# Softmax sums divided in four pieces from a copy, query projection by alternating column halves, and column-half matmuls kept together in the planned order

## Chip, cores and metric

One NeuronCore of one Trainium2 chip runs the whole program; the other cores do nothing. The metric is the device time of one execution in microseconds (us), median over several executions; smaller is better. Nothing of the computation is done on the host.

## What is computed

One step of a two-layer hybrid backbone over 1280 tokens (256 prompt, 1024 sample tokens), model width 1024, all in float32. Each layer makes one input projection, feeds eight heads of latent attention and four heads of a bidirectional gated delta rule, and joins both in one output projection:

```python
mod = jnp.dot(jax.nn.silu(cond), w_ada) + b_ada               # shift, scale, gate
h = rmsnorm(x, norm_w) * (1.0 + scale) + shift
z = jnp.einsum('bsd,de->bse', h, w_in)
q = jnp.einsum('bsr,rf->bsf', rmsnorm(q_lat, q_a_norm), w_qb)  # 8 heads, 64 + 32 wide
kv = jnp.einsum('bsr,rf->bsf', ckv_all, w_kvb)                 # 256 cached + 1024 sample keys
s = (q_nope . k_nope + q_pe . k_pe) * scale
o_a = softmax(s, axis=-1) . v * silu(g_a)
o_b = rmsnorm(o_forward + flip(o_reverse)) * silu(g_b)         # two scans in chunks of 64
x = x + gate * einsum(concat(o_a, o_b), w_out)
```

A scan step computes `v_new = u - w S`, `o = q S + intra v_new`, `S = S*gl + k^T v_new` for each head and direction. A final RMSNorm closes the step; the compressed keys and the scan states are outputs as well.

## The kernel before

**Order.** The program is written as many Python generators ("threads"). `Sched.run` plays them against estimates of each operation's time and always takes the operation that could start first; threads have priorities. What it records is the fixed order of every engine's instructions, so a changed cost or rule moves instructions all over the program. A helper records all operations, so nearly all have line 312 (315 after the change); names tell them apart. Where the plan leaves TensorE idle, `keep_warm` (L178) puts in matmuls that compute nothing, named `spare`.

**Column halves.** A matmul with at most 64 output rows takes a half of TensorE's columns; `Op.half` holds its first output row, 0 or 64 (for the conditioning product `adap` one of four quarters, 0, 32, 64, 96), and is None for a whole one. Once `run` has taken an operation, it goes on with the same thread while the next one's `half` is true and nothing blocks it (L131). `emit` charges 8 ns for a half whose predecessor used another half of the same tile (L267 to L276).

**Stages.** Each layer runs an input projection (`zp`, weights split in high and low parts, three products), in which the delta rule's matrices are prepared, then attention with the scan beside it, then the output projection (`wop`). In one layer's attention stretch every head h has two threads:

- `prep(h)` (L1461) projects keys (`kp`) and queries (`qp`, in `qproj`, L1490: two column blocks j into output rows 0 to 63 and 64 to 127 of one bank, two products k added up for each), takes the scores' maxima (`pm` on TensorE, reductions on VectorE), transposes them (`mxt`), has ScalarE negate them, and sends them through DRAM (`mx_d`) into one row of the query tile. Scores (`sp`) of that head wait for this row.
- `main(h)` (L1555) makes, for each block of 128 keys, the scores (`sp`), their exponentials on ScalarE (`pe`), and the product with the values (`po`), and adds the exponentials up in `acc`. GpSimd does most of these adds and VectorE some, the last one among them. After 2 blocks (prompt) and 10 blocks (sample) it starts a `finish` thread.
- `finish` (L1615) sums `acc` over partitions on TensorE (`pd`), takes the reciprocal into the tile `ob`, multiplies by the gate on GpSimd and by `po` on VectorE, and sends the result away. There are two `ob` tiles. It has 2 × 8 × 2 = 32 calls; half have 512 columns, half 128.

Beside them stand the scan (`ks`, `up`, `su`, `po<-S,kc` on TensorE; `ru`, `S`, `oT` on VectorE and ScalarE), the squares of its output (`jk` on ScalarE), the values of the next pair of heads (`vp` to `vv`), and the splitting of the output weights in high (`woh`, ScalarE) and low (`wol`, GpSimd) parts. In the code below, V is VectorE, S ScalarE, G GpSimd, PE TensorE, SY SyncE.

Of the kernel before, what the change touches and what calls it, by code (L numbers as in the profile page):

```python
# [16 lines left out]
P = 128  # L17
# [14 lines left out]
BLK = ((0, 256), (256, 512), (768, 512))  # L32
# [24 lines left out]
class Sched:  # L57
# [47 lines left out]
    def run(self):  # L105
        while self.th:
# [19 lines left out]
            r, _, t = best  # L126
            if t.q:
                if isinstance(t.q[0], Op):
                    self.t = t.t = max(t.t, t.q[0].start())
                Sched.step(t)  # L130
                while t.q and isinstance(t.q[0], Op) and t.q[0].half and not t.q[0].blocker():  # L131
                    Sched.step(t)
                continue
            t.t, t.wait = r, None
# [87 lines left out]
class Op:  # L222
# [44 lines left out]
    def emit(self):  # L267
        s = self.start()
        if self.eng == "PE":
            n = self.outs[0][0]  # L270
            if (self.half is None) != (Sched.half is None):
                s = max(s, Sched.clk.get("PE", 0.0) + (92 if Sched.half is None else 200))
            if self.half is not None:
                if Sched.half not in (None, (n, self.half)) and Sched.half[0] == n:
                    self.ns = 8
            Sched.half = None if self.half is None else (n, self.half)  # L276
        e = s + self.ns
        if self.eng == "PE":
            Sched.keep_warm(s)
# [115 lines left out]
def body(tc, I, O):  # L395
# [11 lines left out]
    PE, V, S, G, SY = Eng(nc.tensor, "PE"), Eng(nc.vector, "V"), Eng(nc.scalar, "S"), Eng(nc.gpsimd, "G"), Eng(nc.sync, "D")  # L407
# [6 lines left out]
    def bank(name):  # L414
        yield "bank"
        Sched.banks.remove(min(Sched.banks))
        t = pp.pool.tile([P, 512], F32, tag="mm", name=name)
        Sched.span(t)
        return t
# [139 lines left out]
    def mixer(l, hhl):  # L559
# [901 lines left out]
        def prep(h):  # L1461
# [27 lines left out]

            def qproj(bl):  # L1490
                pt = yield from bank("qp")
                for j, b in enumerate(bl):
                    c0, n = BLK[b]
                    for k in range(2):
                        PE.matmul(pt[64 * j : 64 * j + 64, :n], hw[:, k, :], qn[:, k, c0 : c0 + n], start=(k == 0), stop=(k == 1))
                yield 0
                for j, b in enumerate(bl):
                    c0, n = BLK[b]
                    S.copy(at["qr"][0:64, c0 : c0 + n], pt[64 * j : 64 * j + 64, :n])
                free(pt)  # L1500
                for b in bl:
                    c0, n = BLK[b]
# [112 lines left out]
        def finish(h, po, acc, m, c0, n, ga):  # L1615
# [4 lines left out]
            pd = yield from bank("pd")  # L1620
# [1 line left out]
                PE.matmul(pd[64 * x : 64 * x + 64, :n], twos, acc[:, x, :n])  # L1622
            yield 0
            ob = at["ob"][i % 2]
            V.reciprocal(ob[:, :n], pd[:, :n])
            free(pd)
            yield 0
            G.tensor_tensor(ob[:, :n], ga, ob[:, :n], op=ALU.mult)
            yield 0
            V.tensor_tensor(ob[:, :n], po[:, :n], ob[:, :n], op=ALU.mult)  # L1630
# [279 lines left out]
```

## Time and profile before

| what | us |
|---|---|
| median of 3 executions | 2223.09 (2219.53, 2223.09, 2223.38) |
| the profiled execution | 2217.9, of which the span 2216.1 |
| TensorE (PE) busy | 2097.0, 95% of the span, mean granted clock 0.986 |
| VectorE (DVE) busy | 1442.9 |
| GpSimd (POOL) busy | 847.4 |
| ScalarE (ACT) busy | 771.0 |

The span is the time from the first to the last recorded instruction of the profiled execution; 1.8 us of its time lie around it. Busy times are unions of an engine's intervals. Matmul intervals overlap, since they are pipelined. TensorE's records come singly for float32r matmuls and in pairs for float32 ones (`kp`, `qp`, `po`, `pd`, `spare`). The bracket at a timeline row's end gives the engine's idle time before it and what ended it.

### The profile page before, as it was taken

How to read it: one execution, taken by the hardware profiler on the slowest of the kernel's cores; microseconds unless marked ns; L12 is line 12 of the kernel's file. 1: busy time of each engine (PE TensorE's matmuls, PEld its weight loads, DVE VectorE, ACT ScalarE, POOL GpSimd, SP SyncE). 2: the span in 40 equal slices, each digit the busy share in tenths (PEclk: the TensorE clock that was granted, in tenths of full speed). 3: DMA queues.
4: the chain of work that ended last, by engine and by line, in shares of the span. 5: the costliest groups of instructions: out<-in, count | busy, mean ns of one | idle time of the engine just before them, and what ended most of it. 6: DMA issues, size and time to landing. Idle time of an engine off the chain costs nothing. (4 is left out here: it accounts for less than half of the span.)

```text
span 2216.1 us, 35036 instructions
## 1 busy us (share of the span) xinstructions
PE 2097.0 (95%) x12154; PEld 1519.9 (69%) x12154; DVE 1442.9 (65%) x3085; ACT 771.0 (35%) x2120; POOL 847.4 (38%) x757
## 2 busy tenths in 40 slices
PE   8899999989989998999999999998998999899998
PEld 6676778778666654555777777887876665455576
DVE  4767476686585765564667783887749576665454
ACT  4244224242124344443222441433222434544311
POOL 2343222352415247445331442144341524735521
PEclk9999999989999999999999999999999999999999
DMA  7376776856764322101423654677875441310153
GB/s 276 118 240 196 250 223 194 237 168 209 221 168 150 101 83 71 34 18 50 148 101 95 196 163 151 191 219 216 255 248 158 116 136 53 100 33 19 41 161 110
DMA packets 388481, 327.88 MB, mean 148 GB/s; under 512 B 88736, under 2 KB 326784, under 8 KB 388048
## 3 DMA queue, kind: packets, MB, share of 16 engines
q1 hardware_dynamic: 388304, 325.63, 48.9%
q8 instruction: 97, 1.59, 0.3%
q14 instruction: 80, 0.66, 0.1%
HBM read 220.08 MB, written 105.46 MB: 147 GB/s over the span
## 5 line engine op out<-in xcount | busy, mean ns | idle before, releaser
L312 PE MATMUL zp<-hh,wh 128*128 128x512 f32 (+2 forms) x1128 | 421.5, 374 | 8.4 <-DVE ai L312 6.9
L312 PE MATMUL zp<-hh,wl 128*128 128x512 f32 (+2 forms) x1128 | 421.1, 373 | 4.1 <-POOL wl L312 3.8
L312 PE MATMUL zp<-hl,wh 128*128 128x512 f32 (+2 forms) x1128 | 420.6, 373 | 3.2 <-POOL hl L312 3.1
L312 POOL TENSOR_TENSOR wl<-wr,wh 128x512 fp32r<-128x512 f32 (+1 forms) x114 | 156.2, 1370 | 400.8 <-DVE wh L312 231.5
L312 ACT ACTIVATE pe<-sp 128x512 f32<-128x512 f32 (+1 forms) x352 | 201.6, 578 | 259.0 <-PE sp L312 243.5
L312 DVE TENSOR_REDUCE at<-pm 128x1 f32<-128x512 f32 (+1 forms) x336 | 212.3, 683 | 80.2 <-PE pm L312 79.3
L312 POOL TENSOR_TENSOR pe<-pe,pe 128x1024 f32<-128x1024 f32 x96 | 229.3, 2388 | 80.8 <-DVE pe L312 51.4
L312 PEld LDWEIGHTS zp<-hh,wh 128*128 128x128 f32 (+1 forms) x1128 | 214.1, 190 | 41.9 <-DVE ai L312 7.1
L312 PE MATMUL sp<-at 97*128 97x512 f32 (+1 forms) x704 | 239.9, 408 | 2.6 <-ACT pe L312 1.5
L312 PEld LDWEIGHTS zp<-hh,wl 128*128 128x128 f32 (+1 forms) x1128 | 214.0, 190 | 38.0 <-issue 5.6
L312 PEld LDWEIGHTS zp<-hl,wh 128*128 128x128 f32 (+1 forms) x1128 | 214.2, 190 | 36.3 <-POOL hl L312 4.5
L312 PE MATMUL po<-pe,vv 128*64 128x512 f32 (+1 forms) x768 | 187.1, 563 | 3.4 <-ACT pe L312 2.6
L312 PEld LDWEIGHTS sp<-at 97*128 97x128 f32 x704 | 123.3, 189 | 88.5 <-issue 56.1
L312 POOL TENSOR_SCALAR kpt<-ktok,kdb 128x128 f32<-128x128 f32 x160 | 130.0, 824 | 94.1 <-DMA ai_d<-kpt 84.4
L312 PE MATMUL pm<-at 96*128 96x512 f32 (+1 forms) x416 | 129.2, 385 | 7.9 <-ACT at L312 4.6
L312 PE MATMUL sp<-at,at 97*128 97x512 f32 (+1 forms) x352 | 136.5, 388 | 0.0
L312 DVE TENSOR_TENSOR pe<-pe,pe 128x256 f32<-128x256 f32 (+1 forms) x64 | 79.5, 1244 | 83.9 <-POOL pe L312 43.4
L312 PE MATMUL wop<-woh,ol 128*128 128x512 f32 x288 | 114.4, 397 | 2.2 <-POOL ol L312 2.2
L312 PE MATMUL wop<-woh,oh 128*128 128x512 f32 x288 | 114.5, 398 | 0.0
L312 PE MATMUL wop<-wol,oh 128*128 128x512 f32 x288 | 114.3, 397 | 0.0
L312 PEld LDWEIGHTS pm<-at 96*128 96x128 f32 x416 | 70.9, 191 | 61.5 <-ACT pe L312 21.4
L312 DVE TENSOR_TENSOR wtmp<-blk,W 104x31 f32<-104x31 f32 (+15 forms) x248 | 105.6, 426 | 4.6 <-POOL W L312 0.9
(267 smaller groups left out, 3860.7 us busy)
## 6 DMA issues: line engine op xcount, KB each, us to landing
wr<-in_w_main SPq DMA_DIRECT2D x116, 256.0 KB
ti<-ai_d SPq DMA_DIRECT2D x144, 192.0 KB
ai_d<-ai SPq DMA_DIRECT2D x80, 256.0 KB
kc<-kqv_d SPq DMA_DIRECT2D x160, 128.0 KB
wa<-in_w_ada SPq DMA_DIRECT2D x64, 256.0 KB
kqv_d<-yc SPq DMA_DIRECT2D x48, 256.5 KB
kq<-kqv_d SPq DMA_DIRECT2D x16, 641.0 KB
rb<-grow_d SPq DMA_DIRECT2D x80, 128.0 KB
```

What stands on the lines that cost most here:

```text
L312: op = Op(lambda: f(*a, **k), self.key, self.ns(name, a, k, aps), outs, [x for x in aps if x is not acc])
```

## The change

```diff
--- before.py
+++ after.py
@@ -128,7 +128,7 @@
                 if isinstance(t.q[0], Op):
                     self.t = t.t = max(t.t, t.q[0].start())
                 Sched.step(t)
-                while t.q and isinstance(t.q[0], Op) and t.q[0].half and not t.q[0].blocker():
+                while t.q and isinstance(t.q[0], Op) and t.q[0].half is not None and not t.q[0].blocker():
                     Sched.step(t)
                 continue
             t.t, t.wait = r, None
@@ -270,10 +270,13 @@
             n = self.outs[0][0]
             if (self.half is None) != (Sched.half is None):
                 s = max(s, Sched.clk.get("PE", 0.0) + (92 if Sched.half is None else 200))
-            if self.half is not None:
-                if Sched.half not in (None, (n, self.half)) and Sched.half[0] == n:
-                    self.ns = 8
-            Sched.half = None if self.half is None else (n, self.half)
+            if self.half is None:
+                Sched.half = None
+            elif Sched.half and Sched.half[0] == n and self.half not in Sched.half[1]:
+                self.ns = 8
+                Sched.half[1].add(self.half)
+            else:
+                Sched.half = (n, {self.half})
         e = s + self.ns
         if self.eng == "PE":
             Sched.keep_warm(s)
@@ -1489,9 +1492,9 @@
 
             def qproj(bl):
                 pt = yield from bank("qp")
-                for j, b in enumerate(bl):
-                    c0, n = BLK[b]
-                    for k in range(2):
+                for k in range(2):
+                    for j, b in enumerate(bl):
+                        c0, n = BLK[b]
                         PE.matmul(pt[64 * j : 64 * j + 64, :n], hw[:, k, :], qn[:, k, c0 : c0 + n], start=(k == 0), stop=(k == 1))
                 yield 0
                 for j, b in enumerate(bl):
@@ -1622,9 +1625,12 @@
                 PE.matmul(pd[64 * x : 64 * x + 64, :n], twos, acc[:, x, :n])
             yield 0
             ob = at["ob"][i % 2]
-            V.reciprocal(ob[:, :n], pd[:, :n])
+            S.copy(ob[:, :n], pd[:, :n])
             free(pd)
             yield 0
+            for x in range(0, n, P):
+                V.reciprocal(ob[:, x : x + P], ob[:, x : x + P])
+                yield 0
             G.tensor_tensor(ob[:, :n], ga, ob[:, :n], op=ALU.mult)
             yield 0
             V.tensor_tensor(ob[:, :n], po[:, :n], ob[:, :n], op=ALU.mult)
```

Four things change. `run` keeps an operation with half 0 with its predecessor too (0 counted as false before). `emit` charges 8 ns only for a half that the running set has not used yet. `qproj` has the product index outside the block index, so halves alternate 0, 64, 0, 64. `finish` copies the sums to SBUF on ScalarE, frees the bank, and takes the reciprocal there in place, in pieces of 128 columns, between which other threads may go.

Over the whole program TensorE's order gets 50 more `spare` instructions (231 for 181), VectorE's 80 reciprocals of these for 32, ScalarE's 32 copies more; GpSimd's and SyncE's counts stay. The order on every engine is another one. Three places follow.

**GpSimd, layer 0**, late in attention, where a head's adds end; the stretch begins with adds of `pe` into the sum. Before:

```order
L312 TENSOR_TENSOR pe_8841<-pe_8841,pe 128x1024
L312 TENSOR_TENSOR wol_9020<-wor,woh_9019 128x512
L312 TENSOR_TENSOR pe_8841<-pe_8841,pe 128x1024
L312 TENSOR_TENSOR wol_9020<-wor,woh_9019 128x512
L312 TENSOR_TENSOR wol_9035<-wor,woh_9034 128x512 x2
L312 TENSOR_TENSOR wol_9051<-wor,woh_9050 128x512 x2
L312 TENSOR_TENSOR ob_7082<-at_7080,ob_7082 128x512
```

After:

```order
L315 TENSOR_TENSOR pe_9180<-pe_9180,pe 128x1024
L315 TENSOR_TENSOR wol_9193<-wor,woh_9192 128x512
L315 TENSOR_TENSOR pe_9180<-pe_9180,pe 128x1024
L315 TENSOR_TENSOR wol_9224<-wor,woh_9223 128x512 x2
L315 TENSOR_TENSOR wol_9259<-wor,woh_9258 128x512 x2
L315 TENSOR_TENSOR wol_9307<-wor,woh_9306 128x512 x2
L315 TENSOR_TENSOR wol_9364<-wor,woh_9363 128x512 x2
L315 TENSOR_TENSOR ob_7094<-at_7092,ob_7094 128x512
```

Behind the last add stood five `wol` in a row; now there are eight. VectorE's order beside it (adds of `pe`, the next head's maxima `at_6488` from `pm`) was:

```order
L312 TENSOR_TENSOR pe_8841<-pe_8841,pe 128x1024
L312 TENSOR_REDUCE at_6488<-pm 128x1 x4
L312 TENSOR_REDUCE at_6488<-pm 128x2
L312 TENSOR_REDUCE at_6488<-at_6488 128x8
L312 TENSOR_TENSOR pe_8841<-pe_8841,pe 128x1024 x2
```

and now is:

```order
L315 TENSOR_REDUCE at_6488<-pm 128x1
L315 TENSOR_TENSOR pe_9180<-pe_9180,pe 128x1024
L315 TENSOR_REDUCE at_6488<-pm 128x1 x3
L315 TENSOR_REDUCE at_6488<-pm 128x2
L315 TENSOR_TENSOR pe_9180<-pe_9180,pe 128x1024
L315 TENSOR_REDUCE at_6488<-at_6488 128x8
```

The maxima of the next head were all reduced ahead of this head's last two adds; now four reductions stand between these adds and the one that ends the maxima stands behind both.

**TensorE, layer 0**, where one head's scores end and the next head's (`sp` of 256 columns) begin; `mxt` starts the way of the next head's row of maxima. Before:

```order
L312 MATMUL mxt<-ident,at_6488 10x128
L312 MATMUL sp<-at_6486 128x512
L312 MATMUL sp<-at_6486,at_6487 128x512
L312 MATMUL sp<-at_6486 128x512 x2
L312 MATMUL sp<-at_6486,at_6487 128x512
L312 MATMUL po<-pe,vv 64x512 x2
L312 MATMUL sp<-at_6486 128x512 x2
L312 MATMUL sp<-at_6486,at_6487 128x512
L312 MATMUL sp<-at_6486 128x512 x2
L312 MATMUL sp<-at_6486,at_6487 128x512
L312 MATMUL po<-pe,vv 64x512 x4
L433 MATMUL spare<-ident 128x128
L312 MATMUL pd<-pe_10143,twos 64x512 x2
L312 MATMUL sp<-at_7079 128x256 x2
```

After:

```order
L315 MATMUL sp<-at_6486 128x512 x2
L315 MATMUL sp<-at_6486,at_6487 128x512
L315 MATMUL mxt<-ident,at_6488 10x128
L315 MATMUL po<-pe,vv 64x512 x4
L315 MATMUL pd<-pe_10179,twos 64x512 x2
L436 MATMUL spare<-ident 128x128 x5
L315 MATMUL sp<-at_7091 128x256 x2
```

The transposition has moved behind all scores of the old head. Between it and the new head's scores stand `po`, `pd` and five `spare` in place of scores, products and one `spare`.

**ScalarE, layer 1**, the end of the scan, where `jk` squares its output and TensorE wants exponentials (`pe`) and keys (the casts from `kp`). Before:

```order
L312 COPY ru<-up 128x128 x2
L312 ACTIVATE pe<-sp 128x512
L312 ACTIVATE jk,o_19057<-oT 128x128 x9
L312 COPY vv<-vp 128x512
L312 ACTIVATE jk,o_19057<-oT 128x128
L312 COPY vv<-vp 128x512
L312 ACTIVATE pe<-sp 128x512
L312 COPY vv<-vp 128x512
L312 ACTIVATE pe<-sp 128x512
L312 CAST at_17391<-kp 64x384 x2
L312 ACTIVATE pe_19125<-sp 128x2x128
```

After:

```order
L315 COPY ru<-up 128x128 x2
L315 CAST at_17452<-kp 64x384 x2
L315 ACTIVATE jk,o_19171<-oT 128x128 x9
L315 COPY ob_17455<-pd 128x512
L315 ACTIVATE jk,o_19171<-oT 128x128
L315 CAST at_17452<-kp 64x384 x2
L315 ACTIVATE pe_19157<-sp 128x2x128
L315 ACTIVATE pe<-sp 128x2x128
```

And what TensorE has beside it after the change:

```order
L315 MATMUL po<-S_19100,kc 128x128
L315 MATMUL pd<-pe_18600,twos 64x512 x2
L315 MATMUL sp<-at_16839 128x256 x2
L315 MATMUL sp<-at_16839,at_16840 128x256
L315 MATMUL kp<-at_16838,at_16841 64x384 x2
L315 MATMUL sp<-at_16839 128x256 x2
L315 MATMUL sp<-at_16839,at_16840 128x256
L436 MATMUL spare<-ident 128x128 x10
L315 MATMUL po<-pe_19157,vv 64x128 x2
L315 MATMUL po<-pe,vv 64x128 x2
L436 MATMUL spare<-ident 128x128 x10
L315 MATMUL otp<-ident,oT 128x128 x2
```

Ten squares and the copy `ob<-pd` now stand ahead of the exponentials `pe_19157`, which TensorE wants for `po`. The values' copies (`vv`) that stood between the squares are gone from here; two pairs of key casts surround the squares.

## Rows read from the trace of the kernel before

**Rows 1.** Busy time by stretch (stretch, its us; per engine busy, count; PEclk; DMA).

```profile
95.00:620.00 525.00, 495.85 (x3326) 391.41 (x3326) 356.06 (x906) 165.29 (x573) 180.03 (x216) 0.98 0.71 213
620.00:1047.00 427.00, 408.08 (x2120) 245.02 (x2120) 264.19 (x460) 184.19 (x404) 193.78 (x119) 0.99 0.29 82
...
1172.00:1690.00 518.00, 490.77 (x2982) 405.92 (x2981) 373.70 (x944) 167.50 (x573) 188.79 (x224) 0.99 0.65 193
1690.00:2105.00 415.00, 399.06 (x2028) 236.93 (x2028) 257.82 (x439) 176.69 (x386) 190.85 (x117) 0.98 0.27 77
...
844.30:846.30 2.00, 1.98 (x5) 0.37 (x5) 0.30 (x1) 0.00 (x0) 0.00 (x0) 0.50 0.01 4
```

**Rows 2.** Timeline, PE, query projections (start, us; count; idle and releaser in brackets).

```profile
701.99 1.08 PE L312 MATMUL qp<-at,at 128*64 128x256 f32 x4
...
705.99 1.94 PE L312 MATMUL qp<-at,at 128*64 128x512 f32 x8
707.87 0.50 PE L312 MATMUL sp<-at 97*128 97x512 f32 x1
```

**Rows 3.** By line and shape: the reciprocals of DVE and one copy of ACT.

```profile
L312 DVE RECIPROCAL ob<-pd 128x512 f32<-128x512 f32 x16 | 53.7, 3358 | 21.8 <-PE pd L312 21.6
...
L312 DVE RECIPROCAL ob<-pd 128x128 f32<-128x128 f32 x16 | 15.2, 953 | 7.4 <-PE pd L312 7.3
...
L312 ACT COPY vv<-vp 128x512 f32<-128x512 f32 x24 | 13.9, 585 | 17.9 <-PE vp L312 17.9
```

**Rows 4.** Timeline, DVE then PE, layer 1, a division beside the scan.

```profile
1788.29 3.36 DVE L312 RECIPROCAL ob<-pd 128x512 f32<-128x512 f32 x1
1791.56 0.77 DVE L312 SCALAR_TENSOR_TENSOR ru<-ks,neg_eg,vtok 128x128 f32<-128x128 f32 x3
...
1789.06 2.17 PE L433 MATMUL spare<-ident 128*128 128x128 f32 x18
1791.87 1.00 PE L312 MATMUL up<-ru,ti 128*128 128x128 f32 x6 [0.64 <-DVE ru L312]
```

**Rows 5.** Timeline, DVE, POOL, PE: one undisturbed sum, two beside GpSimd.

```profile
1785.81 1.22 DVE L312 TENSOR_TENSOR pe<-pe,pe 128x1024 f32<-128x1024 f32 x1
...
827.97 1.89 DVE L312 TENSOR_REDUCE at<-pm 128x1 f32<-128x512 f32 x3 [1.76 <-PE pm L312]
...
836.90 4.96 POOL L312 TENSOR_TENSOR wol<-wor,woh 128x512 fp32r<-128x512 f32 x4
...
836.98 5.96 DVE L312 TENSOR_TENSOR pe<-pe,pe 128x1024 f32<-128x1024 f32 x1 [6.92 <-POOL pe L312]
...
844.32 1.98 PE L312 MATMUL pd<-pe,twos 128*64 128x512 f32 x4 [5.47 <-DVE pe L312]
...
866.49 3.50 POOL L312 TENSOR_TENSOR at<-at,at 96x512 fp32r<-96x512 f32 x2
...
866.55 2.29 DVE L312 TENSOR_TENSOR pe<-pe,pe 128x1024 f32<-128x1024 f32 x1 [6.29 <-POOL pe L312]
```

**Rows 6.** Timeline, PE and SP: two places where the row of maxima comes back.

```profile
884.05 0.28 PE L312 MATMUL mxt<-ident,at 128*10 128x128 f32 x1
...
888.33 0.48 PE L312 MATMUL sp<-at 97*128 97x256 f32 x2
...
885.96 0.23 SPq L312 DMA_DIRECT2D at<-mx_d  x1
...
737.37 0.27 SPq L312 DMA_DIRECT2D at<-mx_d  x1
...
740.16 0.50 PE L312 MATMUL sp<-at 97*128 97x256 f32 x2 [0.19 <-DMA at<-mx_d]
```

**Rows 7.** Squares of the scan's output on ACT; one PE wait behind them.

```profile
L312 ACT ACTIVATE jk<-oT x80: 293/310/330, 367.6 to 1848.0; 128x128 bf16<-128x128 f32 x80
L312 ACT ACTIVATION_READ_ACCUMULATOR jk<-oT x80: 185/186/208, 367.8 to 1848.2; 128x1 f32 x80
...
1849.40 1.62 PE L312 MATMUL po<-pe,vv 128*64 128x512 f32 x3 [0.48 <-ACT pe L312]
```

## Prediction

> **What bounds the kernel now.** I read first the busy time by stretch, because a mean over the whole hides stages. TensorE is busy in nearly all of every stretch [rows 1]. So another engine's work counts only where TensorE waits for it. The division and the query projection lie in the two attention stretches. There TensorE stands idle 427.0 − 408.1 = 18.9 us in layer 0 and 415.0 − 399.1 = 15.9 us in layer 1, so 34.8 us and the spare matmuls among the busy time are all that a change of waits can win in them. The reader should see how little that is: 1.6% of 2217.9 us. A longer wait has no such ceiling. It also has a second price: after the longest stall of attention the granted clock was 0.50, that is 1.2 instead of 2.4 GHz, for the next 2 us at least [rows 1].
>
> Next comes the timeline at the edited lines, one place each, then the order that the change makes. What changed in it I weigh with durations of before, since the plan's own times are estimates.
>
> **Query projection: 0 (−0.9 to 0).** With one block, four records of 256 columns stand one behind another and take 1.08 us [rows 2]. At that rate eight records of 512 columns would take over 3.5 us. They take 707.87 − 705.99 = 1.88 us [rows 2], up to the start of the scores behind them. So TensorE already works on both column halves at once in the old order 0, 0, 64, 64, and alternating can only trim an edge: at most 0.06 us in each of 16 groups. Here I choose nothing.
>
> **Halves kept together, and the planner's other charge for `adap`: 0 (−4 to +4).** Neither removes an operation. The reshuffled input projections are what they can change. TensorE idles 29.2 us in that stretch of layer 0 and 27.2 us in layer 1 [rows 1]; work of one kind in two orders differs by 2 us there, and I allow twice that.
>
> **The division: −5 (−9.6 to 0).** Sixteen of 3.36 us become 64 pieces at about the 0.95 us that 128 columns take today, and sixteen of 0.95 stay [rows 3]: VectorE works 16 × (4 × 0.95 − 3.36) = 7 us more. ScalarE gets 16 copies of 0.585 and 16 of about half that, 14 us [rows 3]. Both lie off the path: VectorE is idle for 427.0 − 264.2 = 163 us and ScalarE for 427.0 − 184.2 = 243 us of layer 0's attention [rows 1]. What can be won is a wait behind a long division. In layer 1 the division at 1788.29 keeps the scan's `ru` back until 1791.56, and TensorE has only spares and a gap from 1789.06 to 1791.87 [rows 4], 2.81 us. Layer 0's plan has the same situation once. With pieces the scan waits for one of them at most, 0.95 instead of 3.36, so 2.4 us come back in each layer. I take 5, the bound 9.6 if four places do this, and 0 if other threads do not come between the pieces (they stand in order, whatever TensorE needs).
>
> **GpSimd's run in layer 0: +6.2 (−1.2 to +7.5).** In the old order VectorE's last-but-one add of a head began 0.08 us after a run of four `wol` and lasted 5.96 us; the same add undisturbed lasts 1.22 [rows 5]. The run ended at 836.90 + 4.96 = 841.86, the add at 842.94: it came out about 1.1 us after the whole run. TensorE's `pd` waited 5.47 us for it [rows 5]. In the new order eight `wol` stand there; the eighth needs a cast queued on ScalarE behind this head's copy of `pd`, so seven can run on: 7 × 4.96/4 = 8.7, the add about 9.7 us, 3.7 more than now. Behind this add now stand four reductions, 4 × 1.89/3 = 2.5 us [rows 5], in front of the add that `pd` needs. Sum 6.2. All eight `wol` would make it 7.5. The low end comes from the other row: at 866.55 the same add, started just after GpSimd's, got in between two of its operations and took 2.29 us [rows 5]; then 2.29 − 5.96 + 2.5 = −1.2. I take the upper row, since it has the same operands.
>
> The Trainium skill ("SBUF — State Buffer", section "SBUF: two separate sides") has an exclusive lock that the engine which starts first keeps for one whole instruction. By it the add would wait out one `wol` and this term would be about −1, an estimate; the row with four `wol` speaks against that reading, the one at 866.55 for it.
>
> **The row of maxima: +6.5 (4 to 12).** The way from `mxt` to the new head's scores was covered in 4.28 us at 884.05 to 888.33, without a wait; by its pieces, 1.91 to the read's issue there and 2.79 from issue to use at 737.37, where TensorE did wait for it, it is 4.70 [rows 6]. I take 4.4. In the old order eight scores' groups stood between. In the new one `mxt` (0.28), four `po` and two `pd` are left; eight records of such halves take 1.88 [rows 2], four 0.94, together 3.1. That leaves 1.2 to 1.6, less one spare of 0.24 (18 records in 2.17 [rows 4]) that stood there anyway: 1.1 us at each of the four hand-overs where the plan does this, two in each layer, 4.5 in all. In layer 0, behind the long run of `wol`, `mxt` comes after `pd` and only twelve value products cover it, 24 records at 0.12 = 2.9; SyncE's order issues two loads ahead of the read, at least 0.25 us each [rows 6]. So 4.4 + 0.5 − 3.2 = 1.7, say 2, and 5 if the read also queues behind their bytes.
>
> **The squares: +5 (3 to 6).** Ten squares with their read-outs at 0.31 + 0.19 [rows 7], the copy of 0.585 and two casts of about as much now stand before the exponentials that TensorE's next `po` needs: 5.0 + 0.6 + 1.0 = 6.6 us. TensorE has `pd`, six scores of 256 columns and two `kp` in that time, about 3 us. Then `otp` needs the same squares' result by way of GpSimd and VectorE. I put 3.6 for the first and 2 for the second, less the 0.48 that TensorE waits there now [rows 7].
>
> **Sum.** 0 + 0 − 5 + 6.2 + 6.5 + 5 = +12.7; 2217.9 + 12.7 = 2230.6 us for an execution like the profiled one. The median shown is 2223.09, 5.2 above it, with runs on both sides; I add half: **2233 us**, 0.4% over the median.
>
> **Rivals.**
>
> - *Faster, 2214.* The pieces let the scan through and the new waits are covered. For it: the 2.81 us are there [rows 4], and a planned gap need not be one on the chip. Against it: the plan puts in 50 more spares, so it expects more idle time itself. Taking the division at −9.6, GpSimd's run at −1.2 and the waits near +2 gives 2223 − 9 = 2214. It decides at `up`: within 1 us after the last `ks`. Chance 0.17.
> - *No change, 2224.* Gains and waits balance within 0.2% (4.4 us, about what a measurement of this kernel can tell). That is so if VectorE gets in between GpSimd's operations as at 866.55 [rows 5], −1.2 for 6.2, and squares cost 3: 12.7 − 7.4 − 2 = 3.3, and 2217.9 + 3.3 + 2.6 = 2224. The add of 5.96 us speaks against it, that one for it. Chance 0.20.
> - *Column halves run in strict order, 2210.* If records could not overlap before an earlier half had ended, seven of eight records would count in the old order and four in the new: 16 × 3 × 1.88/4 = 23 us less, with the other terms 2233 − 23 = 2210. The 1.88 us nearly exclude it [rows 2]. Chance 0.02. The Trainium skill ("TensorE: Matmul & The Clock Gate", "The mechanism") says that matmuls start and end in program order; the trace has eight in the time of four.
> - *Slower still, 2242.* The small read waits behind the two loads (+3), the squares cost 6 (+1), and three of the new stalls last long enough to bring the clock to 0.50 as at 844.30 [rows 1]: 2 us at half rate lose 1, and I take 1 to 2 each, +5. For it: the stall of 5.47 us did just that [rows 5]. Against it: the plan fills the squares' stall with spares. Chance 0.12.
>
> **How the numbers follow.** Forecast 0.49, rivals 0.17, 0.20, 0.02, 0.12. Faster: 0.17 + 0.02 = 0.19. Same: 0.20. Slower: 0.49 + 0.12 = 0.61. All low ends of the sum give 2217.9 − 0.9 − 4 − 9.6 − 1.2 + 4 + 3 = 2209, all high ends 2217.9 + 4 + 7.5 + 12 + 6 = 2247; with the runs' own spread the forecast's own range is 2226 to 2242. The one given, 2212 to 2250, takes in the faster case and the slower.
>
> **What would show it.** In the changed profile: `qp` with eight records still 1.9 us; four pieces near 0.95 us with `ru` between some; the add beside eight `wol` near 9.7 us and `pd` behind it idle over 8; idle before the new head's first scores about 1 us with the read of `mx_d` as its end; `po` after the squares waiting 3 us for ScalarE. Wrong if that add takes under 3 us, if `qp` halves its time, or if the two attention stretches got shorter.

## The result and the profile after

The changed kernel takes 2236.03 us (median of 5 executions, 2232.36 to 2245.78), the kernel before 2221.82 (median of 5, 2216.97 to 2223.38): a ratio of 1.0073 with a 95% interval of 1.0046 to 1.0100. It is slower, as forecast: 2233 was predicted, in a range of 2212 to 2250. A second measurement gave 2240.71 us and a ratio of 1.0092 (1.0068 to 1.0116).

The first lines of the page of the changed kernel:

```profile
span 2235.1 us, 35358 instructions
...
PE 2114.4 (95%) x12254; PEld 1532.4 (69%) x12254; DVE 1466.4 (66%) x3133; ACT 784.4 (35%) x2152; POOL 851.6 (38%) x757
```

The profiled execution took 2236.86 us, of which the span is 2235.1: 19.0 more than the span before. TensorE's busy time grew by 17.4 us, without one useful matmul more, so busy time says nothing here; one has to ask what kept it busy and at what clock.

The busy time by stretch of the changed kernel answers [rows 1]. The first two rows are the attention of layer 0 and of layer 1 (from the last `zp` matmul to the first `wop` one), the others lie in layer 0's:

```profile
621.10:1051.60 430.50, 404.69 (x2122) 243.69 (x2120) 267.45 (x461) 189.46 (x418) 192.05 (x118) 0.98 0.29 84
1696.20:2112.40 416.20, 401.59 (x2105) 238.01 (x2103) 271.01 (x487) 188.46 (x414) 193.41 (x118) 0.99 0.29 83
...
874.80:884.20 9.40, 0.05 (x1) 0.00 (x0) 9.40 (x7) 0.00 (x0) 4.71 (x4) 0.68 0.00 0
884.20:888.00 3.80, 3.74 (x13) 2.16 (x14) 1.11 (x3) 1.25 (x3) 0.40 (x1) 0.50 0.01 1
...
892.40:896.30 3.90, 0.04 (x2) 0.06 (x1) 0.00 (x0) 0.00 (x0) 0.00 (x0) 0.87 0.92 257
896.30:900.00 3.70, 3.70 (x16) 2.72 (x17) 0.43 (x1) 0.77 (x2) 0.00 (x0) 0.50 0.41 97
```

The same view of the kernel before, with the same two boundaries:

```profile
623.70:1035.30 411.60, 393.98 (x2062) 235.44 (x2060) 252.82 (x443) 183.15 (x401) 190.73 (x118) 0.99 0.29 84
1675.80:2092.80 417.00, 398.43 (x2046) 237.12 (x2044) 262.45 (x466) 181.58 (x399) 188.83 (x118) 0.98 0.29 83
```

So in this pair of executions the whole loss lies in one stretch: layer 0's attention went from 411.6 to 430.5 us (+18.9), layer 1's from 417.0 to 416.2. What lies outside adds up to 1387.5 before and 1388.4 after. The other executions of the table below keep the first of these differences and not the second: layer 1's attention takes 416.2 to 421.4 us in the five with the changed order there (after, after again, 1, 2, 4; mean 419.5) and 417.0 and 414.1 in the two of the old order, so it is longer too, by about 4 us.

Timeline of the changed kernel, PE, DVE, POOL and SP, at the places that the prediction spoke of:

```profile
734.47 1.94 PE L315 MATMUL qp<-at,at 128*64 128x512 f32 x8
736.34 0.49 PE L315 MATMUL up<-ru,ti 128*128 128x128 f32 x2
...
871.78 3.07 PE L436 MATMUL spare<-ident 128*128 128x128 f32 x26
884.26 1.97 PE L315 MATMUL pd<-pe,twos 128*64 128x512 f32 x4 [9.41 <-DVE at L315]
886.16 0.38 PE L315 MATMUL mxt<-ident,at 128*10 128x128 f32 x1
...
896.28 0.77 PE L315 MATMUL sp<-at 97*128 97x256 f32 x2 [3.86 <-DMA at<-mx_d]
...
936.83 0.27 PE L315 MATMUL mxt<-ident,at 128*10 128x128 f32 x1
...
941.09 0.49 PE L315 MATMUL sp<-at 97*128 97x256 f32 x2
...
1867.77 2.40 PE L436 MATMUL spare<-ident 128*128 128x128 f32 x20
1871.19 0.71 PE L315 MATMUL po<-pe,vv 128*64 128x128 f32 x8 [1.03 <-ACT pe L315]
1871.83 2.50 PE L436 MATMUL spare<-ident 128*128 128x128 f32 x20
1874.47 0.44 PE L315 MATMUL otp<-ident,oT 128*128 128x128 f32 x2
...
870.95 9.64 DVE L315 TENSOR_TENSOR pe<-pe,pe 128x1024 f32<-128x1024 f32 x1
880.51 2.47 DVE L315 TENSOR_REDUCE at<-pm 128x1 f32<-128x512 f32 x4
882.90 1.21 DVE L315 TENSOR_TENSOR pe<-pe,pe 128x1024 f32<-128x1024 f32 x1
...
870.88 8.62 POOL L315 TENSOR_TENSOR wol<-wor,woh 128x512 fp32r<-128x512 f32 x7
887.60 1.27 POOL L315 TENSOR_TENSOR wol<-wor,woh 128x512 fp32r<-128x512 f32 x1 [8.09 <-ACT woh L315]
...
887.04 0.31 SPq L315 DMA_DIRECT2D mx_d<-at  x1
888.89 0.33 SPq L315 DMA_DIRECT2D gbc<-gate_d  x1
889.28 0.98 SPq L315 DMA_DIRECT2D x<-in_x  x1
890.31 0.28 SPq L315 DMA_DIRECT2D at<-mx_d  x1
```

Read in the order of time. GpSimd runs seven `wol`, VectorE's add that began 0.07 us behind them lasts 9.64 us, four reductions and the last add follow, and `pd` stands idle for 9.41 us ([rows 5]: 5.96 and 5.47). The granted clock is then 0.50, the lower of its two levels. `mxt` sets the row of maxima going; SyncE issues two loads of 512 KB (`gbc` and `x`) ahead of the read, and the new head's scores wait 3.86 us for it, 10.12 us after `mxt` ([rows 6]: 4.28). In those 3.9 us the DMA engines are 92% busy at 257 GB/s: the read sits behind the loads' bytes. After this stall too the clock is 0.50.

The reciprocals by shape ([rows 3]: 3358 ns for 512 columns, 953 for 128 straight from the bank):

```profile
L315 DVE RECIPROCAL ob<-ob 128x128 f32<-128x128 f32 x80 | 70.2, 921 | 40.1 <-ACT ob L315 40.1
```

### The profile page after: what moved, and what is told of

It reads as the page before. It is cut to its first block, busy times and chain, and to the rows that moved or that the text cites. A ratio compares the mean times of both kernels' runs of the same rounds, so it can differ in the third digit from the quotient of the medians.

```text
span 2235.1 us, 35358 instructions
## 1 busy us (share of the span) xinstructions
PE 2114.4 (95%) x12254; PEld 1532.4 (69%) x12254; DVE 1466.4 (66%) x3133; ACT 784.4 (35%) x2152; POOL 851.6 (38%) x757
## 5 line engine op out<-in xcount | busy, mean ns | idle before, releaser
L315 DVE TENSOR_TENSOR pe<-pe,pe 128x256 f32<-128x256 f32 (+1 forms) x64 | 92.1, 1440 | 99.9 <-POOL pe L315 83.8
```

Source lines behind the costliest of these rows:

```text
L315: op = Op(lambda: f(*a, **k), self.key, self.ns(name, a, k, aps), outs, [x for x in aps if x is not acc])
```

## Experiments

Each was timed against the kernel before on the same chip. "Attention 0" and "attention 1" are the stretches cut as above from one profiled execution, "rest" is the remainder of its span, "add" the longest of VectorE's 64 adds of `pe`. The kernels that are numbered 1 to 5 and named in the rows below are explained behind the table.

| kernel | median us | ratio (95%) | attention 0 | attention 1 | rest | add us |
|---|---|---|---|---|---|---|
| before | 2221.82 | | 411.6 | 417.0 | 1387.5 | 5.96 |
| before again | 2219.52 | 0.9998 (0.9981 to 1.0014) | 411.7 | 414.1 | 1390.2 | 5.96 |
| after | 2236.03 | 1.0073 (1.0046 to 1.0100) | 430.5 | 416.2 | 1388.4 | 9.64 |
| after again | 2240.71 | 1.0092 (1.0068 to 1.0116) | 434.0 | 419.8 | 1392.1 | 9.64 |
| 1 row first | 2238.58 | 1.0072 (1.0047 to 1.0097) | 427.2 | 421.4 | 1392.6 | 9.63 |
| 2 row first, short run | 2236.22 | 1.0068 (1.0046 to 1.0089) | 427.2 | 420.0 | 1389.4 | 4.73 |
| 3 old query projection | 2244.27 | 1.0100 (1.0074 to 1.0126) | 427.0 | 417.7 | 1388.2 | 9.63 |
| 4 small loads first, short run | 2233.28 | 1.0048 (1.0030 to 1.0066) | 418.1 | 420.3 | 1396.3 | 4.74 |
| 5 one reciprocal | 2244.46 | 1.0102 (1.0086 to 1.0119) | 430.6 | 421.2 | 1388.7 | 9.62 |
| division alone | 2235.77 | 1.0061 (1.0046 to 1.0076) | 409.8 | 427.1 | 1399.9 | 7.38 |
| query projection alone | 2233.69 | 1.0049 (1.0033 to 1.0065) | 428.4 | 413.4 | 1387.9 | 8.40 |
| planner's rules alone | 2220.57 | 0.9997 (0.9981 to 1.0013) | 420.3 | 409.7 | 1389.4 | 3.54 |
| the charge alone | 2219.23 | 0.9996 (0.9977 to 1.0014) | 412.3 | 411.8 | 1385.7 | 4.72 |
| before, short runs, scan first | 2225.05 | 1.0015 (1.0002 to 1.0029) | 416.6 | 415.4 | 1387.6 | 5.94 |

The rest varies between 1388.2 and 1396.3 in the seven executions whose order outside the attention stretches is the same (after, after again, 1 to 5), so a stretch is compared with its like, and a few us of the whole say little. Numbers 1 to 5 keep the plan of the changed kernel and move or replace instructions only when they are recorded, so that one difference stands alone (the first line is a scheme of what each kernel fills in):

```diff
+    HOLD = [(names of operations, name of another one)]
...
-        self.call()
+        Sched.out(self)
```

`out` records an operation at once, unless HOLD lists it: then it is recorded behind the other one.

**After again.** The same kernel, to have it on the chip of the next three.

> The changed kernel once more, as the base for the edits of this call. Expected 2233 to 2239 us; in its profile the sum of the exponentials in layer 0 that lasted 9.64 us and the 9.41 us of idle time before the sums over partitions (pd) come again within 0.5 us, since both follow from the fixed order. If they do not come again, they were an accident of one execution and the cause lies elsewhere.

Layer 0's attention is 434.0 us this time, layer 1's 419.8; `pd` idles 9.42 us, the scores idle 4.39 for the row of maxima. Both stalls come again, as they should if the order makes them. The length of the second is not fixed by the order, though: it is 1.47 us in number 3 and 1.82 in number 5, which leave the loads and the read where they are.

**1. Row first.** The two loads go behind the read.

```diff
+    HOLD = [(['D gbc_9507<-gate_d_103', 'D x<-in'], 'D at2<-mx_d0_4')]
```

> Only SyncE's order differs from the changed kernel: in layer 0 the read of the row of maxima stands ahead of the two loads (gbc and x) it stood behind. Theory (the row waits behind these loads, in the queue and then for their bytes): the way from the transposition mxt to the new head's scores falls from 10.12 to 4.3 to 4.9 us, TensorE's 3.86 us of idle time there vanish and half of the spares' 2.23 us do, and with the clock kept up the kernel is 4 to 7 us faster than the changed one. Rival (the row is late for another reason, as bytes of the weights loaded earlier): the way stays over 8 us, 0 to 1 us faster. Rival (the cost is spread over the program): the wait falls, but turns up at the next one, 0 to 2 us faster.

From `mxt` to the scores it is now 5.85 us and no idle time: the loads alone had cost 10.12 − 5.85 = 4.3. But TensorE's next want is a weight whose load stands behind the same loads (timeline, PE, of this kernel):

```profile
897.63 0.87 PE L341 MATMUL kp<-at,at 128*64 128x384 f32 x4 [1.09 <-DMA at<-in_w_hd]
```

Attention 0 is 3.3 us shorter than in the first profile, but 427.0 also came out for number 3, where nothing of this was changed and the stall happened to be 1.47 us. The local wait is shown gone; of the 4 to 7 us expected in the total nothing is resolved (1.0072 against 1.0073 and 1.0092).

**2. Row first, short run.** As 1, and four of the seven `wol`, with the casts (`woh`) of these and of a fifth, go behind ScalarE's step on `mxt`, so that two of the seven still run behind the head's last sum.

```diff
-    HOLD = [(['D gbc_9507<-gate_d_103', 'D x<-in'], 'D at2<-mx_d0_4')]
+    HOLD = [(['D gbc_9507<-gate_d_103', 'D x<-in'], 'D at2<-mx_d0_4'),
+            (['S woh5_9258<-wor_9262', 'S woh5_9258<-wor_9290',
...
+              'G wol6_9307<-wor_9310', 'G wol6_9307<-wor_9333'], 'S at4<-mxt')]
```

> As e1_row_first, and nine casts and subtractions of the output weights in layer 0 (woh and wol of the rows 5 to 7) stand behind ScalarE's step on mxt, so that GpSimd has two subtractions instead of seven behind its last sum. Theory (VectorE's sum waits out GpSimd's whole run): the sum lasts 2 x 1.24 + 1.1 = 3.6 us instead of 9.64, pd starts 6 us sooner, and the kernel is 10 to 14 us faster than the changed one, 4 to 7 of that from the row. Rival (the sum waits out one instruction at most, and was long for another reason): the sum stays over 8 us, and the time is that of e1_row_first within 2 us. Rival (work put off comes back): the sum is short, but the subtractions then hold back the gate's product on GpSimd and the values' copies on ScalarE, and half of the 6 us are lost again: 7 to 10 us faster than the changed one.

Timeline of this kernel, DVE and PE:

```profile
869.81 3.52 DVE L341 TENSOR_TENSOR pe<-pe,pe 128x1024 f32<-128x1024 f32 x1
...
877.00 1.97 PE L341 MATMUL pd<-pe,twos 128*64 128x512 f32 x4 [3.30 <-DVE at L341]
...
890.12 0.44 PE L341 MATMUL pd<-pe,twos 128*64 128x128 f32 x4 [2.29 <-DVE pe L341]
894.39 1.55 PE L341 MATMUL kp<-at,at 128*64 128x384 f32 x4 [3.83 <-DMA at<-in_w_hd]
```

The add takes 3.52 us behind two `wol` instead of 9.64 behind seven, and `pd` idles 3.30 instead of 9.41. That settles what held it: GpSimd's run. Yet of the 10 to 14 us expected nothing comes out at the end (1.0068). Six `wol` now stand ahead of the gate's product on GpSimd, VectorE's `ob` behind that, the prompt's add behind `ob`: its `pd` waits 2.29 us. And `kp`, now earlier by 7.6 us than in the changed kernel, finds its weights not there, 3.83 us. The waits went on to the next resource.

**3. Old query projection.** The second and third of the four `qp` calls trade places again; the plan stays.

```diff
+        if n.startswith("qp_"):
+            c = Sched.seen[n] = Sched.seen.get(n, 0) + 1
+            if c == 2 and op.half == 64:
+                Sched.late = op
+                return
+            if c == 3:
+                op.call()
+                Sched.late.call()
+                return
```

> Only the order of the query projection's four matmuls is taken back in the changed kernel's program: halves 0, 0, 64, 64 in place of 0, 64, 0, 64, all else in the same place. Theory (both halves run at once in either order): 8 records still take 1.88 us, the time is that of the changed kernel within 0.2%, a mean difference of 0 to 1 us. Rival (strict order of columns' halves): 8 records take 3.3 us or more, 16 groups, 20 us slower than the changed kernel.

Timeline of this kernel, PE, the group that stands at 734.47 in the changed kernel:

```profile
734.63 1.94 PE L351 MATMUL qp<-at,at 128*64 128x512 f32 x8
736.50 0.49 PE L351 MATMUL up<-ru,ti 128*128 128x128 f32 x2
```

Eight records to the next matmul: 1.87 us in the order 0, 0, 64, 64, and 736.34 − 734.47 = 1.87 in the order 0, 64, 0, 64. The alternation itself is worth nothing. The totals (1.0100 here, 1.0092 with it) agree within their intervals.

**4. Small loads first, short run.** The two loads go further back, behind the next head's weights, gates and query rows; `wol` as in 2.

```diff
-    HOLD = [(['D gbc_9507<-gate_d_103', 'D x<-in'], 'D at2<-mx_d0_4'),
+    HOLD = [(['D gbc_9507<-gate_d_103', 'D x<-in'], 'V ob1<-po'),
```

> As e2_row_first_short_run, but the two large loads (gbc, x) stand behind all the small ones of the next head (its weights, rotary rows and gates), which e2 had left behind them, and where its key projection waited 3.83 us. Theory (in layer 0 three waits stand in a row, the sum behind GpSimd's run, the row of maxima and the next head's weights behind the same two loads; taking away only the first lets the next one end later): the wait of 3.83 us goes, pd waits about 3.3 us, the stretch from the fourth mxt to the sixth is 6 to 9 us shorter than the changed kernel's 111.8, and the time 5 to 9 us less than the changed one's. Rival (those loads are late for the bytes of other transfers): the key projection still waits over 2 us, and the time is that of e2 within 2 us.

Timeline of this kernel, DVE and PE:

```profile
872.14 3.52 DVE L341 TENSOR_TENSOR pe<-pe,pe 128x1024 f32<-128x1024 f32 x1
...
879.33 1.08 PE L341 MATMUL pd<-pe,twos 128*64 128x512 f32 x4 [3.29 <-DVE at L341]
...
886.91 0.48 PE L341 MATMUL sp<-at 97*128 97x256 f32 x2
...
891.56 0.44 PE L341 MATMUL pd<-pe,twos 128*64 128x128 f32 x4 [1.34 <-DVE pe L341]
```

Now `kp` waits for nothing, and the gain stays: attention 0 is 418.1 us, against 430.5, 434.0, 427.0 and 430.6 in the four executions with the unchanged order of loads and `wol` (after, after again, 3 and 5; the mean is 430.5): 12.4 us. Of these, TensorE's idle time gives 8.5 (16.6 us against a mean of 25.1), spares 0.4, and 3.5 come from useful work that takes less time, as less of it runs at the lower clock (6.8 us of the stretch are at 0.50, 17.1 to 30.7 in the four). Not all of this is the edit's: `pd`'s four records take 1.08 us here and 1.97 in number 2, behind the same order and the same wait of 3.3 us. The total, 1.0048, lies below the 1.0092 of the changed kernel with intervals that don't meet, and overlaps that of the first comparison. It is still slower than before: these waits, with the clock that goes with them, explain two thirds of that stretch's loss, by one execution of this kernel.

**5. One reciprocal.** The copy stays, the four pieces become one instruction of 512 columns where the first stood; the reciprocals of 128 columns stay.

```diff
-                V.reciprocal(ob[:, x : x + P], ob[:, x : x + P])
+                V.reciprocal(ob[:, x : x + P], ob[:, x : x + P], whole=ob[:, :n])
```

`whole` makes the first piece's call take all of it and drops the other three.

> The changed kernel with one reciprocal of 512 columns in place of each four pieces, at the first piece's place; all else keeps its place. Theory (pieces let the scan through, worth 5 us): scan updates wait again for up to 2.4 us in the two places where pieces are interleaved, 2 to 5 us slower than the changed kernel. Rival (the scan is not held up since the new order has put it elsewhere; what pieces cost is only 16 x 0.4 us of VectorE off the path): 0 to 1 us either way.

1.0102 (1.0086 to 1.0119) lies above the changed kernel's 1.0073 and 1.0092, but the intervals meet, so the total does not settle what the pieces are worth. The places do. Timeline of this kernel, DVE and PE, beside the scan in layer 0, then behind the squares in layer 1:

```profile
784.39 3.35 DVE L349 RECIPROCAL ob<-ob 128x512 f32<-128x512 f32 x1
...
787.96 0.49 PE L349 MATMUL ks<-S,kc 128*128 128x128 f32 x2 [0.99 <-DVE oT L349]
...
1868.83 3.35 DVE L349 RECIPROCAL ob<-ob 128x512 f32<-128x512 f32 x1 [2.71 <-ACT ob L349]
...
1874.28 2.54 DVE L349 TENSOR_TENSOR oT<-oT,o 128x1280 f32<-128x1280 f32 x1 [2.08 <-POOL o L349]
...
1876.88 0.44 PE L349 MATMUL otp<-ident,oT 128*128 128x128 f32 x2 [3.33 <-DVE oT L349]
```

In layer 1 `otp` waits 3.33 us that it doesn't wait with pieces (1874.47 above, without a bracket): the square's small product `o` on VectorE comes out behind the whole reciprocal, GpSimd's power and `oT` behind it. In layer 0 it is the scan that waits: its `oT` and `ru` stand behind the reciprocal, with pieces between them, and `up` starts 7.59 us behind the scores at 782.78, against 5.59 in the changed kernel (783.07 to 788.66); up to the next `qp` the difference is 2.6 us. So where an operation that TensorE needs stands behind the division, pieces win about 3 us in either place, as argued; but the two places are of the new order, and not those that the prediction read.

**Parts of the change on the kernel before.** Four kernels take one part of the diff each, and their planner decides anew: the division; the query projection; both planner's rules; the charge in `emit` alone.

```diff
-            V.reciprocal(ob[:, :n], pd[:, :n])
+            S.copy(ob[:, :n], pd[:, :n])
...
+            for x in range(0, n, P):
+                V.reciprocal(ob[:, x : x + P], ob[:, x : x + P])
+                yield 0
```

> The kernel before with the division's change alone. Its plan has three subtractions at most (not eight) behind a head's last sum on GpSimd, and scores of the old head between mxt and the new head's scores in layer 0. Theory (the loss hangs on these places of the plan, the division itself wins 5 us in the scan): 2 to 6 us faster than the kernel before. Rival (the copy on ScalarE and the seven more microseconds on VectorE cost time themselves): 5 us or more slower than the kernel before.

This is a miss. Attention 0 did shorten, by 1.8 us, but attention 1 grew by 10.1 and the rest by 12. I had read the plan of layer 0 alone. (The plan is the order of the instructions that the scheduler makes.) In layer 1 it has what the whole change has in layer 0 (timeline of this kernel, POOL, DVE and PE):

```profile
1902.72 7.40 POOL L312 TENSOR_TENSOR wol<-wor,woh 128x512 fp32r<-128x512 f32 x6
...
1903.83 7.38 DVE L312 TENSOR_TENSOR pe<-pe,pe 128x1024 f32<-128x1024 f32 x1
...
1914.27 1.98 PE L312 MATMUL pd<-pe,twos 128*64 128x512 f32 x4 [6.87 <-DVE at L312]
```

Six `wol`, an add of 7.38 us, `pd` idle for 6.87. The division adds no such work: it only changes what the planner puts there. The 12 us of the rest are not explained by this.

```diff
-                for j, b in enumerate(bl):
-                    c0, n = BLK[b]
-                    for k in range(2):
+                for k in range(2):
+                    for j, b in enumerate(bl):
+                        c0, n = BLK[b]
```

> The kernel before with the query projection's loops exchanged alone. The planner's old charge makes another plan of it: eight subtractions stand behind a head's last sums in layer 0, and in both layers mxt stands right ahead of the old head's last products. Theory (the plan's places cost, not the order of the halves): 4 to 14 us slower than the kernel before, with a sum of over 8 us beside GpSimd's run in layer 0. Rival (alternating halves help by themselves): as fast as before or faster.

As expected. Two swapped lines that cost nothing by themselves (number 3) make the kernel 0.5% slower; attention 0 is 16.8 us longer, and there the plan makes a run again and an add lasts 8.40 us.

```diff
-                while t.q and isinstance(t.q[0], Op) and t.q[0].half and not t.q[0].blocker():
+                while t.q and isinstance(t.q[0], Op) and t.q[0].half is not None and not t.q[0].blocker():
```

That line goes with the charge in `emit`, as in the diff of the whole change, and then the charge alone:

> The kernel before with the two edits of the scheduler alone, division and query projection as before. Its plan has five subtractions in a row behind a head's last sum in layer 0, the long divisions, and in both layers one head whose mxt stands behind its sums with only twelve value products to cover the row. Theory (plan's places decide): a sum of about 5 x 1.24 + 1.1 = 7.3 us there, 2 to 10 us slower than before. Rival (the scheduler's edits are a gain that the division or the query projection spoils): faster than before by 2 us or more.

For both rules this is a miss: no difference, 0.9997. Attention 0 is 8.7 us longer, attention 1 is 7.3 shorter.

> The kernel before with the planner's new charge for column halves alone (emit), everything else as before. Read by the places, its plan is the mildest of all: three subtractions behind a head's last sum in layer 0, scores of the old head behind mxt in every head of both layers from the third on, and 144 spares instead of 181. Theory (the plan's places decide): both attention stretches at or below the 411.6 and 417.0 us of before, none of the sums over 5 us, 2 to 8 us faster than before. Rival (the places do not decide; every plan but the one of before is slower, as three of four new plans so far): 5 to 14 us slower, with attention stretches longer by waits of another kind.

The charge alone is a miss as well: 0.9996. Two rows of the tile `pe` on DVE (min, median and max in ns) show the longest add; first of the query projection alone:

```profile
L312 DVE TENSOR_TENSOR pe<-pe,pe x64: 360/1216/8397, 684.5 to 2108.3; 128x1024 f32<-128x1024 f32 x48, 128x256 f32<-128x256 f32 x16
```

then both planner's rules alone:

```profile
L315 DVE TENSOR_TENSOR pe<-pe,pe x64: 360/1220/3540, 678.5 to 2098.8; 128x1024 f32<-128x1024 f32 x48, 128x256 f32<-128x256 f32 x16
```

The plans with an add over 7 us (whole change, division, query projection) are the slow ones, those with 3.54 to 5.96 the fast ones. That is six plans (with the old one) and a pattern, not a proof: number 2 shortened the add and won nothing.

**Before again, and before with short runs and the scan first.** The first is the old kernel as it is. The second keeps the old plan, puts the `wol` of the runs behind the gate's product in both layers, and has the division at 734.49 and 1788.29 wait until the three `ru` are done, as pieces were to allow.

```diff
+    HOLD = [(['G wol2_9035<-wor_9036', 'D wor<-in_w_out', 'G wol2<-wor', 'G wol3<-wor'], 'G ob1<-at6'),
+            (['G wol1_19376<-wor_19381', 'D wor<-in_w_out', 'G wol1<-wor', 'G wol2<-wor', 'G wol3<-wor'], 'G ob1<-at6'),
+            (['V ob1_7082<-pd_8154'], 'V ru<-ks', 3), (['V ob1_17394<-pd_18481'], 'V ru<-ks', 3)]
```

> The kernel before once more, for a second profile. In its two attention stretches the waits are fixed by the order, so 411.6 and 417.0 us come again within 1.5 us, with sums of 5.96 and 4.71 us beside GpSimd's runs. The second input projection took 511.6 us in the first profile, and 513 to 520 us in seven profiles of the changed order: if it comes out at 514 or more here, that difference is the spread of executions and not the change's; if it stays under 512.5, some 4 us of the change's loss lie there.

> The kernel before, with its places of the same kinds mended by order alone: GpSimd multiplies by the gate ahead of four output-weight subtractions in each layer, so that one of them stands behind a head's last sum in place of four and three, and the two divisions that held the scan back stand behind the three scan updates. Theory (sums wait out GpSimd's run; the scan waits for the division): the sums take about 1.2 + 1.1 = 2.3 us instead of 5.96 and 4.71, pd waits 2.4 to 3.6 us less in each layer, up starts 2 to 2.8 us sooner in each scan, and the kernel is 8 to 13 us faster than before, its attention stretches about 6 and 5 us shorter. Rival (the waits come back at the next place, as in layer 0 of the changed kernel when only its run was shortened): 0 to 4 us faster. Rival (work that is put off holds back the gates or the weights' loads): slower.

The old kernel repeats to 0.02%. Its attention 0 came again (411.7), its attention 1 did not within the 1.5 us expected (414.1 for 417.0). The second input projection, which was to tell spread from loss, took 513.5 us (511.6 in the first profile, 513.1 to 519.9 in the seven of the changed order), between the two signs set for it; some 3 us of the change's loss may lie there.

The second kernel is no faster, 1.0015 (1.0002 to 1.0029), though each edit did its local work: the two adds take 2.30 and 2.27 us, `pd` idles 1.76 and 2.73 instead of 5.47 and 5.26. Its `up` in layer 1 came 0.8 us sooner behind `pd` (3.90 for 4.70 us), but the new head's scores only 0.1 sooner (7.80 for 7.91): they now waited 0.55 us for the product `ob`, which the late division had put off. In layer 0 `up` came 0.9 sooner and the scores 0.3, with 1.01 us of waiting for the row of maxima. How soon `up` could come this does not show: the nine `spare` instructions that the old plan put ahead of it (18 records, 2.17 us) stay in the order, and `up` starts as they end. And the work moved from one run met another add (timeline, DVE, POOL, PE):

```profile
864.84 5.93 DVE L342 TENSOR_TENSOR pe<-pe,pe 128x1024 f32<-128x1024 f32 x1 [9.89 <-POOL pe L342]
...
864.77 2.48 POOL L342 TENSOR_TENSOR at<-at,at 96x512 fp32r<-96x512 f32 x2
867.21 2.47 POOL L342 TENSOR_TENSOR wol<-wor,woh 128x512 fp32r<-128x512 f32 x2
...
871.43 0.80 PE L342 MATMUL pm<-at 96*128 96x256 f32 x2 [7.16 <-DVE at L342]
```

Four GpSimd instructions, 5.93 us, and 7.16 idle at `pm`, where the old order has 2.29 and no stall [rows 5]. No kernel of the study is faster than the old one beyond its interval.

## Why the prediction was right

Time and sign came out, and the stall that was to carry the largest cost is there at its size. Not every term held, and part of the agreement is luck. The sum was +12.7 us for an execution like the profiled one; the profiled pair differs by 19.0, the medians by 14.2 and 19.1. The clock and a part of the row of maxima came on top of the sum, and against them went waits in layer 1 that no term named.

- **GpSimd's run in layer 0: +6.2 forecast, +6.8 found.** The add 9.64 (9.7 forecast), the four reductions 2.47 (2.5). From the end of the useful work to `pd` it is 9.41 idle and 2.9 of spares, 12.3, against 5.5. Number 2 shows the cause by taking five `wol` out: 3.52 and 3.30. The seven instructions are waited out whole. The Trainium skill ("SBUF — State Buffer", section "SBUF: two separate sides") has a lock that is held for one whole instruction. Had the add come in when the first `wol` ended, as one does at 857.96 in the same profile (2.30 us), it would have ended some 7 us sooner: here the measurement decides.
- **The row of maxima: +6.5 forecast, +8.7 found, distributed otherwise.** Behind the long run I took 2 us, 5 at most; it cost 3.86 idle and 2.2 spare against 0.3 before, 5.8. The working had the loads' issue as its cost and their bytes only as a bound; numbers 3 and 5, with 1.47 and 1.82 idle, would have given 2.0 to 2.4 less. Also SyncE issued the first load at 888.89, 1.85 after the write; the profile has it wait for the eighth `wol` (887.60 to 888.87). The four hand-overs I put at 1.1 each cost about 0.7: `mxt` to scores is 941.09 − 936.83 = 4.26 us there (and so at 1020.04, 1997.71 and 2080.88), 1.07 of it with spares alone and nothing idle, against 0.35 with spares alone at four places before. The spares stand where the useful work is missing and just cover the way.
- **The squares: +5 forecast, about +5.5 found.** 2.40 of spares and 1.03 idle ahead of `po` (3.6 forecast), 2.50 of spares ahead of `otp` (2 forecast), less the 0.48 of before. They were not tried alone, so that the squares are the cause is argued from the order and not shown.
- **The clock, in no term of the sum but in the rival at 2242: about +5.7.** 0.50 at 884.20 to 888.00 and after 896.30 to beyond 900. The useful work of layer 0's attention, the union of its intervals without spares, takes 392.6 us instead of 386.8; that the lower clock makes all of this is read, not tried.
- **The query projection: 0 forecast, 0 found** (number 3); strict order of the halves is out.
- **The division: −5 forecast; its size shows, but not at the places named.** Pieces do let the scan through in layer 0 of the changed kernel, and without them 2.6 and 3.3 us are lost at two places (number 5). That "2.4 us come back in each layer" at the two divisions of the old order is not shown: with `ru` out of their way (last experiment) the next head's scores came 0.1 and 0.3 us sooner, with the old plan's spares still ahead of `up`.
- **The halves kept together: 0, ±4.** Layer 0's input projection did not move beyond its own spread; layer 1's may be some 3 us longer (see "before again"), within the bound.

Sum for layer 0: 6.8 + 5.8 + 1.4 + 5.7 = 19.7, against 18.9 measured. In layer 1 the squares and two hand-overs cost about 6.9. The stretch is 0.8 shorter in the first pair and 4 longer in the means (419.5 for 415.6), so 3 to 8 us came back: `pd` idles 3.88 us for 5.26, a wait of 1.18 at `pm` and that of 0.64 at `up` beside a division [rows 4] are gone, and waits of about half a us behind ScalarE, while waits of 1.62 at another `pm` and 1.02 at an `mxt` are new. I did not part these by experiment: with another plan all come at once.

Still open: why the rest varies by 8 us between executions of one order, whether the division alone lengthens it (by 12 against the first profile, by 4 against the longest of the changed order), and what lies in attention 0 of the planner's rules alone, where the clock's mean is 0.97 without a long add.

## What to carry to other kernels

Where a planner sets the order, the cost of an edit is that of the new plan: read it in every layer for runs of GpSimd work that start just ahead of a VectorE sum which TensorE waits for, before counting what the edit itself saves. A wait that is removed shows up at the next resource in the chain (here sum, row of maxima, weights, in this order), and only the removal of all three moved the stretch clearly. Compare stretches, not totals: a local gain of 12 us was plain in its stretch and blurred by others in the whole.

## What was unexpected of the hardware

- A VectorE add with two inputs in SBUF that began 0.07 us after GpSimd's run waited out all seven of its instructions, 9.64 us; behind six 7.38 (it began 1.11 after them), behind four 5.93 to 5.96, behind two 3.52. Of runs longer than two I had a row for four only. It is no fixed rule. In the changed kernel's own profile the add at 857.96 came in after the first instruction (2.30 us), and GpSimd's second, of 1.29 us in other places, then lasted 2.25; and at one place of layer 1 (1909.91 in the first profile) the same order of three `wol` gave an add of 3.52 us, which came in after two, in the first profile and in number 3, and of 4.73 (after all three) in after again, 1, 2, 4 and 5. What decides, no run here shows.
- A read of 5 KB behind two loads of 512 KB took 5.97 us from its issue to its first use (2.79 without them, [rows 6]), and this is not constant: in four executions of the same order around it TensorE stood idle for it 3.86, 4.39, 1.47 and 1.82 us.
- The eight `qp` records take 1.87 us in either order of the column halves, in the same position of the same plan.
